# Four mod steps in the router of layer 0, f32r routing weights and tokens, and expert weights in 1 MB transfers of two rows per partition

## The chip, the cores and the metric

The kernel runs on one core of a Trainium2 chip. The time is the device time of one execution in microseconds, and what counts is the median of several runs: 1551.51 us over three runs (1550.75 to 1552.95) before the change.

## The reference, cut to what matters

A diffusion backbone of two layers over 256 latent tokens `x` and 256 context tokens `ctx`, with D = 1024. Layer 0 mixes tokens by windowed attention, layer 1 by differential attention, and behind each stands a hierarchical mixture of 32 experts (4 groups of 8, the best two in the best group). Layer 0 works on all 512 tokens, layer 1 needs the 256 latent ones alone. Shift, scale and gate of every sub-layer (`mod`) are products of `silu(c)` and `silu(c_ctx)` with `mod_w`.

```python
mod  = (silu(c)     @ mod_w[i] + mod_b[i]).reshape(B, 6, 1, D)     # modc from c_ctx
h = rmsnorm(x, norm_g[i, 1]) * (1 + mod[:, 4]) + mod[:, 3]
lg = t @ wg + bg                       # 4 groups
le = t @ we + be                       # 32 experts
top_p, top_i = top_k(softmax(le of the best group), 2)
wts = p_grp * top_p / sum(top_p)
u = xblk @ w_up[e]                     # w_up[e] is 1024 x 1024
y = (silu(u[:, :512]) * u[:, 512:]) @ w_down[e]      # w_down[e] is 512 x 1024
out[token] += wts * y
x = x + mod[:, 5] * out
```

All inputs are float32. The expert weights are 2 x 32 x 6.3 MB, all of which are read, whatever the routing is.

## The kernel before, in words

**Memory.** SBUF holds an arena of 43 slots of 128 x 1024 f32 (4 KB per partition each). `Slot` hands them out, the longest free first. `Stream.one` (L171 to 178) takes a slot and issues the next entry of `plan` as a DMA of 512 KB on SP's queue. SP runs ahead of the work: its next DMA waits until the slot's last reader is through, and until the DMA eight before it (they share eight semaphores in turn) has landed. So the order of `plan` is the order of the transfers, and how far they run ahead is the number of slots that the rest of the kernel leaves.

**The order of work.** TensorE's instructions stand in the order in which the code issues them (a manual schedule for that engine); the other engines get theirs from a scheduler at build time. What each engine does is then a fixed list, and it waits at the head of its list.

**Mod steps.** `mod_step` (L353 on, matmuls at L370) multiplies two k-tiles of one third of `mod_w` for `c` and `c_ctx`: four DMAs of 512 KB and 16 records of matmuls. Four steps make one third, then `mod_finish` copies the sums out of PSUM, transposes them and adds the bias. Layer 0's attention runs through 24 turns; every third of them carries a mod step (`MODS`), so eight steps lie there; the last four belong to the first third of layer 1 and stand in `plan` ahead of the attention's output weights `win_w_o`.

**The router.** `Post` normalises the tokens, transposes them to rows (`flip`, L917 and L925 to L929) and computes the logits (L950). `moe` (L982) then forms on VectorE, one short instruction behind the other (L990 to L1013), the 0/1 matrix `Mb` of token and expert. TensorE turns it into ranks (L1018) and counts (L1024); `key` (L1020) is the place of each token at its expert, 64 places (CAP) for each.

**A pair of experts.** 16 pairs per layer run through the same stages. `gather` (L1126): `P` (L1129) is the one-hot matrix of 128 places; two times `half` (L1152) multiplies `P` with the tokens, 512 features each; in layer 0 the tokens lie as two f32r parts (hi, lo), so that a half is 8 matmuls (4 tiles by 2 parts), in layer 1 as plain f32 (2 matmuls in two passes each, 4 records; `WHOLE`). L1168 transposes `P` for the way back. `gather_weights` (L1188) multiplies `P` in f32 with the routing weights `WR`, and VectorE copies the two or three columns out of PSUM (L1191, L1193). `spread_tokens` (L1198) transposes the gathered tokens, and L1200 adds the shift of `mod`. `up` (L1209) is 64 matmuls of 128 x 512 per pair, `gate` (L1216 to L1218) the SwiGLU, `turned` (L1240) its transpose, `down` (L1252) 32 matmuls, `weigh` (L1277, L1278) scales the output, and `combine` (L1291) with `gated_add` (L509) spreads the pair before back over the tokens while `up` runs. The last pair's `down_last` (L1264) is cut by columns, so that its output can be normalised and stored as it comes. At pair 5 a branch (L1085) asks whether an expert got more than 64 tokens; its other path does not run here.

In layer 0 the experts' stream has 31 slots, in layer 1 39. A pair's weights are 24 DMAs: 12.58 MB.

## Time and profile before

| | |
|---|---|
| median of 3 runs | 1551.51 us (1550.75 to 1552.95) |
| the profiled execution | 1550.44 us, of which its span 1548.8 us |
| TensorE busy | 1458.1 us (94%), granted clock 0.981 in the mean |
| VectorE, ScalarE, GpSimd busy | 42%, 25%, 12% |
| chain of work that ended last | TensorE above all; its costliest lines are L1209 and L1252 |
| bytes moved | 485.67 MB, mean 314 GB/s |
| layer 0, attention | to about 277 us |
| layer 0, router, then its 16 pairs | 282 to 300, then to about 815 us |
| layer 1, `up` of its first pair, of its last | from 1061.85 us, from 1507.87 us |

The span is that of the instructions; all times of rows count from its start. A row of the timeline gives the start, the length and the first and last words of a run of like instructions; "[8.10 <-DVE Mb L1013]" behind one is the idle time of its engine just ahead of it and what ended it. A length overlaps the next row's start where matmuls follow closely, so a stage is read from start to start.

### The profile page before, as it was taken

Reading aid. Unit: us, or ns where it says so; the run is one execution under the profiler, and the core shown is the slowest. Engines: PE = TensorE matmul, PEld = TensorE weight load, DVE = VectorE, ACT = ScalarE, POOL = GpSimd, SP = SyncE. Lnnn points to the kernel's source line nnn. Section 1 sums busy time; section 2 is a strip of 40 time slices with the busy share of each in tenths; the row PEclk is TensorE's granted clock in tenths of the full one; section 3 lists DMA queues with packets and bytes.
Section 4 is the critical chain, followed back from the end, with each engine's and each line's share of the span. In section 5 each row is a group of like instructions: output and inputs, shape, how many; then the busy total and the mean of one; then the engine's idle time right before and its main releaser. Section 6 shows DMA issues by size and latency. Waiting matters only on the chain. (4 is left out here: it accounts for less than half of the span.)

```text
span 1548.8 us, 20271 instructions
## 1 busy us (share of the span) xinstructions
PE 1458.1 (94%) x7463; PEld 800.3 (52%) x7463; DVE 655.5 (42%) x1585; ACT 384.6 (25%) x823; POOL 184.2 (12%) x147
## 2 busy tenths in 40 slices
PE   6998999799999999999999899798999899999997
PEld 4765567445444454444545678684434333433444
DVE  3338862424333443333448726863323222322323
ACT  4426653211010011101115235652101010110112
POOL 2314551000000000000006463100000000000000
PEclk9999999899999999999998999999999999999999
DMA  9767225799989999999996532488999999999991
GB/s 330 243 214 273 82 86 187 278 366 401 395 343 393 401 398 398 391 397 403 382 297 229 182 124 71 161 284 304 387 409 409 409 408 409 409 409 409 409 394 68
DMA packets 169695, 485.67 MB, mean 314 GB/s; under 512 B 20825, under 2 KB 41586, under 8 KB 169586
## 3 DMA queue, kind: packets, MB, share of 16 engines
q1 hardware_dynamic: 169088, 483.66, 82.2%
q8 instruction: 63, 1.03, 0.3%
q10 hardware_dynamic: 498, 0.60, 0.1%
q14 instruction: 46, 0.38, 0.1%
HBM read 483.16 MB, written 1.05 MB: 313 GB/s over the span
## 5 line engine op out<-in xcount | busy, mean ns | idle before, releaser
L1209 PE MATMUL ps<-slotf,row 128*64 128x512 f32 x2048 | 449.2, 593 | 2.1 <-DVE row L1200 2.1
L1209 PEld LDWEIGHTS ps<-slotf,row 128*64 128x64 f32 x2048 | 145.2, 137 | 289.7 <-issue 274.4
L1252 PE MATMUL ps<-slotf,row 128*64 128x512 f32 x960 | 212.6, 595 | 0.0
L546 PE MATMUL ps<-slotr,slotr 128*128 128x512 f32 x768 | 193.4, 405 | 13.4 <-DVE slotf L1414 6.7
L509 DVE SCALAR_TENSOR_TENSOR slotf<-ps,mod,slotf 128x256 f32<-128x256 f32 x408 | 167.3, 477 | 62.3 <-PE ps L1291 29.7
L546 PEld LDWEIGHTS ps<-slotr,slotr 128*128 128x128 f32 x768 | 145.1, 194 | 50.4 <-DVE slotf L1414 7.1
L1252 PEld LDWEIGHTS ps<-slotf,row 128*64 128x64 f32 x960 | 66.3, 137 | 124.9 <-issue 118.9
L1216 ACT ACTIVATE row<-ps 128x512 f32<-128x512 f32 x30 | 17.9, 597 | 425.9 <-PE ps L1209 386.6
L1217 DVE SCALAR_TENSOR_TENSOR row<-row,ps 128x512 f32<-128x512 f32 x30 | 20.6, 687 | 234.4 <-ACT row L1216 234.3
L1278 DVE SCALAR_TENSOR_TENSOR row<-ps,ty,row 128x512 fp32r<-128x512 f32 x60 | 45.0, 750 | 176.5 <-ACT row L1277 173.3
L1277 ACT ACTIVATE row<-ps,ty 128x512 fp32r<-128x512 f32 x60 | 41.3, 688 | 263.0 <-PE ps L1252 262.7
L1291 PE MATMUL ps<-row,row 128*128 128x512 f32 (+1 forms) x512 | 104.4, 348 | 1.1 <-DVE slotf L509 1.0
L1291 PEld LDWEIGHTS ps<-row,row 128*128 128x128 f32 x512 | 77.3, 189 | 36.5 <-ACT row L1216 21.1
L521 POOL TENSOR_TENSOR slotr<-slotf,slotr 128x1024 fp32r<-128x1024 f32 x32 | 78.9, 2479 | 86.9 <-ACT slotr L517 72.1
L1200 DVE TENSOR_TENSOR row<-ps,mod 128x512 f32<-128x512 f32 x64 | 42.7, 686 | 101.7 <-PE ps L1198 100.9
L481 POOL TENSOR_TENSOR row<-row,row 128x512 f32<-128x512 f32 (+1 forms) x13 | 15.0, 1156 | 575.6 <-PE ps L1291 519.4
L1152 PE MATMUL ps<-slotf,row 128*128 128x512 f32 x128 | 65.0, 632 | 7.0 <-PEq L1085 4.7
L1152 PE MATMUL ps<-slotr,row 128*128 128x512 f32 x256 | 70.4, 419 | 0.0
L517 ACT ACTIVATE slotr<-slotf 128x1024 fp32r<-128x1024 f32 x44 | 45.9, 1055 | 63.1 <-DMA slotf<-in_diff_w_qkv 38.0
L1152 PEld LDWEIGHTS ps<-slotr,row 128*128 128x128 f32 x256 | 47.9, 198 | 10.0 <-issue 0.8
L1377 PE MATMUL ps<-slotr,slotr 128*128 128x512 f32 x192 | 47.6, 399 | 0.0
L1198 PE MATMUL ps<-ident,row 128*128 128x128 f32 x256 | 37.8, 280 | 7.5 <-DVE row L1156 6.7
(314 smaller groups left out, 1526.8 us busy)
## 6 DMA issues: line engine op xcount, KB each, us to landing
slotf<-in_moe_w_up SPq DMA_DIRECT2D x512, 512.0 KB, 9.5
slotf<-in_moe_w_down SPq DMA_DIRECT2D x256, 512.0 KB, 10.2
slotf<-in_mod_w SPq DMA_DIRECT2D x96, 512.0 KB, 6.3
slotf<-in_diff_w_qkv SPq DMA_DIRECT2D x24, 512.0 KB, 3.9
slotf<-in_win_w_qkv SPq DMA_DIRECT2D x12, 512.0 KB, 5.2
slotf<-in_win_w_o SPq DMA_DIRECT2D x8, 512.0 KB, 4.0
slotf<-in_diff_w_o SPq DMA_DIRECT2D x8, 512.0 KB, 4.1
slotf<-in_x SPq DMA_DIRECT2D x2, 512.0 KB, 4.1
```

What stands on the lines that cost most here:

```text
L509: ve.scalar_tensor_tensor(xT[k][:, sl], ps[:, sl], g[:, k, r:r + 1], xT[k][:, sl], op0=OP.mult, op1=OP.add)
L517: se.activation(hv, v, AF.Copy)
L521: (eng or (ge if split_i[0] % 3 == 0 else ve)).tensor_tensor(lv, v, hv.bitcast(F32), op=OP.subtract)
L546: pe.matmul(ps[t], h[:, x, ts], w[y][:, kk, :], start=(k + kk == 0 and n == 0), stop=(k + kk == KT - 1 and n == 2))
L1152: pe.matmul(g, P[:, t, :] if len(tok[t]) > 1 else P[:, t, :].bitcast(F32), v[:, hs], start=(t == 0 and i == 0), stop=(t == nt - 1 and i == ...
L1200: ve.tensor_tensor(o.rearrange("p (k c) -> p k c", k=4), ps.rearrange("p (k c) -> p k c", k=4), mods[l][:, 3, 4 * h:4 * h + 4, 0:1].to_bro ...
L1209: pe.matmul(u[h][64 * s:64 * s + 64, :], st["xt"][k // 4][:, c0:c0 + 64], w[s][1][:, h * 512:(h + 1) * 512], start=(k == 0), stop=(k == KT ...
L1252: pe.matmul(y[h][64 * s:64 * s + 64, :], acT[:, c0:c0 + 64], w[s][1][:, h * 512:(h + 1) * 512], start=(k == 0), stop=(k == 3))
L1277: se.activation(yh, y[h], AF.Copy, scale=wsl)
L1278: ve.scalar_tensor_tensor(yl, y[h], wsl, yh.bitcast(F32), op0=OP.mult, op1=OP.subtract)
L1291: pe.matmul(out, part[:, c * 128:(c + 1) * 128], st["PT"][:, :T], start=(i == 0), stop=(i == 1))
L1377: pe.matmul(ps, w[x][:, k % 4, ms], oT0[k][1][:, y, :], start=(k == 0 and i == 0), stop=(k == KT - 1 and i == 2))
```

## The change

1. **Mod steps.** Four of the eight steps in layer 0's attention move into layer 0's router: three behind the logits and one around the counts (`mods_meanwhile`, `last_mods`), with the sums copied by ScalarE and turned after pair 0's gather. In `plan` the output weights now come ahead of these steps' 16 DMAs.
2. **Tokens in two parts.** Layer 1's tokens too are kept as two f32r parts, so a half of the gather is 4 f32r matmuls there. Its eviction needs a second part, on VectorE (L1009 of the new file), and two more slots.
3. **Routing weights in two parts.** `WR` and the token scale are kept as hi and lo in f32r; one pass of `P` gives both parts, and ScalarE adds them as it copies them out (`add_parts`).
4. **Expert weights.** One DMA brings 1 MB into two neighbouring slots: each partition gets 8 KB that lie in a row in HBM, the rows 8p + k (k = 2j, 2j + 1) of `w_up`, or 4p + k of `w_down`. The partitions' rows are 32 KB apart in `w_up` and 16 KB in `w_down`. (Before, each partition got one row of 4 KB, and 128 partitions read 512 KB in a row.) To match, the token's features are dealt to the k-tiles by 8 (`dealt`, `deal` in the evictions), `gate` writes its output with the columns dealt by 4, and the shift is turned by a transpose, a matmul and some short VectorE instructions per layer (`turned_shift`). `up` and `down` fetch for two k and free both slots after the second. The last pair's `w_down` stays in 512 KB DMAs by columns.
5. **Slots** are handed out so that neighbours stay together. The masks take one slot until the end of attention 0. The stream in layer 0 then has 15 pairs of slots, in layer 1 18.

```diff
-WHOLE = ((), (0, 1))
+WHOLE = ((), ())
...
-MODS = range(0, 24, 3)
+MODS = range(0, 24, 6)
...
     def plan_experts(l):
         for p in range(NE // 2):
-            for k in range(KT):
+            for j in range(KT // 2):
                 for s in range(2):
-                    plan.append((a["moe_w_up"][l, 2 * p + s, k * 128:(k + 1) * 128, :], (1024,)))
...
+                    w = a["moe_w_up"][l, 2 * p + s].rearrange("(p k) n -> p (k n)", k=KT)
+                    plan.append((w[:, j * 2048:(j + 1) * 2048], (2, 1024), True))
+            if p + 1 < NE // 2:
+                for j in range(2):
+                    for s in range(2):
+                        w = a["moe_w_down"][l, 2 * p + s].rearrange("(p k) n -> p (k n)", k=4)
+                        plan.append((w[:, j * 2048:(j + 1) * 2048], (2, 1024), True))
...
+    while len(todo) > KT // 2:
+        plan_mod(*todo.pop(0))
+    plan_out(a["win_w_o"][0])
     while todo:
         plan_mod(*todo.pop(0))
-    plan_out(a["win_w_o"][0])
     plan_experts(0)
...
-                cs = slice(ks[0] * 128, (ks[-1] + 1) * 128)
-                hs = slice(h * 512 + ks[0] * 128, h * 512 + (ks[-1] + 1) * 128)
+                src = deal(ps[:, ks[0] * 128:(ks[-1] + 1) * 128])
+                hs = 4 * h + ks[0], len(ks)
+                raw = dealt(self.slots[t][-1].f(), *hs)
                 if t < 2 and len(self.tok[t]) > 1:
...
+                    if self.nr == 1:
+                        ri = self.ri[:, t:t + 1]
+                        se.activation(hi, src, AF.Copy, scale=ri)
+                        ve.scalar_tensor_tensor(lo, src, ri, hi.bitcast(F32), op0=OP.mult, op1=OP.subtract)
...
+    def mods_meanwhile():
+        while len(mod_steps) > 1:
+            mod_step("A")
...
         with tc.manual_schedule(engines=PE):
             lg = post.logits()
+            mods_meanwhile()
...
+        moved = last_mods() if mod_steps else None
...
-                pe.matmul(wps[:, 0:1], P[:, t, :].bitcast(F32), ri[:, t:t + 1], start=(t == 0), stop=(t == nt - 1))
-                ve.tensor_copy(st["w"][:, 1:2], wps[:, 0:1])
+                    pe.matmul(wps[:, 0:2], P[:, t, :], ri[:, t, :], start=(t == 0), stop=(t == nt - 1))
+                add_parts(st["w"][:, 1:2], wps[:, 0:2])
...
+    def add_parts(dst, src):
+        n = src.shape[0]
+        se.activation(tiny("ap", [128, 2], bufs=2)[:n], src, AF.Copy, accum_out=dst)
+
     def gather_weights(P, WR, p, st, n):
...
-            pe.matmul(wps[:, 0:n], P[:, t, :].bitcast(F32), WR[:, t, p, 0:n], start=(t == 0), stop=(t == nt - 1))
+            pe.matmul(wps[:, 0:2 * c], P[:, t, :], WR[:, t, p], start=(t == 0), stop=(t == nt - 1))
...
-            ve.tensor_copy(st["w"][pb, 0:1], wps[pb, s:s + 1])
+            add_parts(st["w"][pb, 0:1], v[pb, s])
...
     def up(st, u, k):
-        w = [stream.next() for _ in range(2)]
+        if k % 2 == 0:
+            st["w_up"] = [stream.next() for _ in range(2)]
+        w = st["w_up"]
...
-        for s in range(2):
-            w[s][0].free()
+        if k % 2:
+            for s in range(2):
+                w[s][0].free()
```

The order of instructions is set at build time, so it can be read for both kernels. **TensorE in the router of layer 0.** The first list is the kernel before, from the last transpose of the tokens (`slotf` is a tile of them) over the logits to the ranks; `before_b` and `ones_b` are constants, `Mb` comes from VectorE.

```order
L917 MATMUL ps_2603<-ident,slotf_111 128x128
L950 MATMUL ps_2651<-ident,row_2633 128x36 x4
L1018 LDWEIGHTS before_b
L1018 MATMUL ps_2702<-Mb_2700,before_b 128x32
L1018 LDWEIGHTS ones_b
L1018 MATMUL ps_2702<-Mb_2700,ones_b 128x32
```

The next two are the changed kernel at the same place: its logits (L1037) with the first matmuls behind them, and the last ones ahead of the ranks (L1121). L419 is the matmul of a mod step, its first name the sums, its second a slot of `mod_w`.

```order
L1000 MATMUL ps_2613<-ident,slotf_65 128x128
L1037 MATMUL ps_2661<-ident,row_2643 128x36 x4
L419 MATMUL ps_2671<-slotf_91,slotf_69 32x512
L419 MATMUL ps_2671<-slotf_93,slotf_69 32x512
L419 MATMUL ps_2671<-slotf_111,slotf_69 32x512
```

```order
L419 MATMUL ps_2671<-slotf_59,slotf_69 32x512
L419 MATMUL ps_2671<-slotf_61,slotf_69 32x512
L419 MATMUL ps_2671<-slotf_95,slotf_69 32x512
L1121 LDWEIGHTS before_b
L1121 MATMUL ps_2749<-Mb_2747,before_b 128x32
```

Between the logits and the ranks there now stand 25 matmuls of mod steps, the last of which reads a fourth step's slot; seven more stand behind the counts.

**SP at the start of layer 0's experts.** Before, the transfers of the output weights and the first of the experts' (`in_moe_w_up`) alternate:

```order
L177 DMA slotf_81<-in_win_w_o 128x4x256
L177 DMA slotf_89<-in_moe_w_up 128x1024
L177 DMA slotf_81<-in_moe_w_up 128x1024
L177 DMA slotf_77<-in_moe_w_up 128x1024
L177 DMA slotf_83<-in_win_w_o 128x4x256
L177 DMA slotf_83<-in_moe_w_up 128x1024
```

and in the changed kernel the tail of the moved steps' weights (`in_mod_w`) stands around the first wide slot (`slotw`):

```order
L217 DMA slotf_89<-in_mod_w 128x2x512
L217 DMA slotf_73<-in_mod_w 128x2x512
L217 DMA slotw_197<-in_moe_w_up 128x2048
L217 DMA slotf_59<-in_mod_w 128x2x512
L217 DMA slotf_61<-in_mod_w 128x2x512
L217 DMA slotf_95<-in_mod_w 128x2x512
L217 DMA slotf_97<-in_mod_w 128x2x512
L217 DMA slotw_190<-in_moe_w_up 128x2048
```

The mod weights of the third step (`slotf_59`, `slotf_61`) and of the fourth (`slotf_95`, `slotf_97`) are issued behind that wide transfer, whose slots are free when attention 0's output product is done.

**VectorE in the router of layer 1.** Before, from the search for the best two to `Mb` and `key`:

```order
L1005 MAX_INDEX s_8330<-s_8329,row_8286 128x8 x2
L1006 TENSOR_SCALAR s_8331<-s_8330 128x16
L1010 TENSOR_TENSOR row_8286<-idx_211,s_8331 128x64
L1011 TENSOR_TENSOR row_8337<-idx_211,s_8331 128x64
L1013 TENSOR_TENSOR Mb_8340<-row_8286,row_8337 128x64
L1020 SCALAR_TENSOR_TENSOR key_8346<-ps_8342,Mb_8340 128x64
```

and changed:

```order
L1108 MAX_INDEX s_8282<-s_8281,row_8234 128x8 x2
L1109 TENSOR_SCALAR s_8283<-s_8282 128x16
L1009 SCALAR_TENSOR_TENSOR slotr_74<-ps_8239,ri_8210,slotr_72 128x8x64
L1009 SCALAR_TENSOR_TENSOR slotr_86<-ps_8246,ri_8210,slotr_84 128x8x64
L1009 SCALAR_TENSOR_TENSOR slotr_74<-ps_8253,ri_8210,slotr_72 128x8x64
L1009 SCALAR_TENSOR_TENSOR slotr_86<-ps_8260,ri_8210,slotr_84 128x8x64
L1113 TENSOR_TENSOR row_8234<-idx_271,s_8283 128x64
L1114 TENSOR_TENSOR row_8289<-idx_271,s_8283 128x64
L1116 TENSOR_TENSOR Mb_8292<-row_8234,row_8289 128x64
```

The four evictions of the tokens' second part stand ahead of the three instructions that end in `Mb`.

## Rows read from the trace of the kernel before

**Rows 1.** The page's line of TensorE: busy time, share of the span, instructions.

```profile
PE 1458.1 (94%) x7463; PEld 800.3 (52%) x7463; DVE 655.5 (42%) x1585; ACT 384.6 (25%) x823; POOL 184.2 (12%) x147
```

**Rows 2.** Busy time of each engine in four stretches: attention 0, the router of layer 0, pairs of layer 0, pairs of layer 1. Columns: the stretch and its length, then busy time and count of TensorE's matmuls, of its weight loads, of VectorE, ScalarE and GpSimd, the granted clock (1.00 is the higher of TensorE's two levels), and the DMA engines' busy share and rate in GB/s.

```profile
155.00:203.00 48.00, 48.00 (x342) 28.39 (x340) 39.36 (x110) 30.12 (x94) 25.82 (x24) 1.00 0.23 78
282.00:300.40 18.40, 8.06 (x48) 6.57 (x47) 14.62 (x60) 5.46 (x11) 2.52 (x2) 0.63 0.70 273
325.00:781.00 456.00, 449.39 (x2160) 215.67 (x2157) 170.81 (x379) 52.95 (x85) 0.00 (x0) 0.99 0.99 388
1100.00:1500.00 400.00, 387.77 (x1861) 166.54 (x1858) 117.72 (x247) 45.34 (x82) 0.00 (x0) 1.00 1.03 409
```

**Rows 3.** All matmuls of mod steps as one group (busy time, mean ns, idle time ahead), and TensorE's timeline in attention 0 at the start of two steps that follow each other (start, length, line, operands).

```profile
L370 PE MATMUL ps<-slotf,slotf 128*32 128x512 f32 x192 | 30.4, 599 | 0.0
```

```profile
179.96 1.04 PE L370 MATMUL ps<-slotf,slotf 128*32 128x512 f32 x2
...
191.89 1.05 PE L370 MATMUL ps<-slotf,slotf 128*32 128x512 f32 x2
```

**Rows 4.** TensorE's timeline from the ranks of layer 0 (the idle time ahead of them begins behind the logits) to the first `up`.

```profile
291.02 0.18 PE L1018 MATMUL ps<-Mb,before_b 128*128 128x32 bf16 x1 [8.10 <-DVE Mb L1013]
...
292.65 1.84 PE L1142 MATMUL ps<-ri,row 128*128 128x1 f32 x8 [1.09 <-DVE s L1031]
294.35 3.76 PE L1152 MATMUL ps<-slotr,row 128*128 128x512 f32 x8
...
300.38 1.94 PE L1209 MATMUL ps<-slotf,row 128*64 128x512 f32 x8 [0.78 <-DVE row L1200]
```

**Rows 5.** TensorE's timeline at the end of attention 0's output product, and SP's timeline of DMA issues around it (start, stretch over which they were issued, count).

```profile
275.21 2.32 PE L1377 MATMUL ps<-slotr,slotr 128*128 128x512 f32 x9
```

```profile
242.49 20.59 SPq L177 DMA_DIRECT2D slotf<-in_moe_w_up  x11
```

**Rows 6.** TensorE's timeline in one pair of layer 0, and the next pair's `down`.

```profile
615.70 7.09 PE L1252 MATMUL ps<-slotf,row 128*64 128x512 f32 x32
...
640.96 0.95 PE L1188 MATMUL ps<-WR,row 128*128 128x3 f32 x8
641.77 2.09 PE L1152 MATMUL ps<-slotr,row 128*128 128x512 f32 x8
644.16 0.63 PE L1168 MATMUL ps<-ident,row 128*128 128x128 f32 x4 [0.30 <-DVE ty L1193]
...
647.45 1.94 PE L1252 MATMUL ps<-slotf,row 128*64 128x512 f32 x8
```

**Rows 7.** VectorE's and ScalarE's timeline at the same place.

```profile
640.78 2.83 DVE L509 SCALAR_TENSOR_TENSOR slotf<-ps,mod,slotf 128x256 f32<-128x256 f32 x7
643.53 0.31 DVE L1191 COPY ty<-ps 64x1 f32<-64x1 f32 x2
643.86 0.16 DVE L1193 COPY ty<-ps 128x1 f32<-128x1 f32 x1
```

```profile
644.13 0.69 ACT L1162 ACTIVATE row<-ps,ty 128x512 f32<-128x512 f32 x1 [5.23 <-DVE ty L1193]
```

**Rows 8.** TensorE's timeline in one pair of layer 1, and the next pair's `up`.

```profile
1092.90 13.90 PE L1209 MATMUL ps<-slotf,row 128*64 128x512 f32 x64
...
1108.75 1.88 PE L1152 MATMUL ps<-slotf,row 128*128 128x512 f32 x4
...
1111.38 1.98 PE L1152 MATMUL ps<-slotf,row 128*128 128x512 f32 x4
...
1114.14 1.09 PE L1198 MATMUL ps<-ident,row 128*128 128x128 f32 x8 [0.44 <-DVE row L1156]
...
1122.09 2.31 PE L1209 MATMUL ps<-slotf,row 128*64 128x512 f32 x10
```

**Rows 9.** The router of layer 1: TensorE's timeline from the ranks to the first half of the gather, a short ScalarE instruction behind it; and from layer 0 a VectorE instruction of the form of the four new ones.

```profile
1055.04 0.18 PE L1018 MATMUL ps<-Mb,before_b 128*128 128x32 bf16 x1 [2.46 <-DVE Mb L1013]
...
1056.20 3.46 PE L1152 MATMUL ps<-slotf,row 128*128 128x512 f32 x4 [0.89 <-DVE s L1031]
```

```profile
1056.26 0.21 ACT L1036 ACTIVATE s<-s 128x8 f32<-128x8 f32 x1 [2.30 <-DVE s L1035]
```

```profile
295.33 0.75 DVE L974 SCALAR_TENSOR_TENSOR slotf<-slotf,s,slotf 128x512 f32<-128x512 f32 x1
```

**Rows 10.** DMA traffic of two stretches: 1100 to 1500 us (expert weights, rows of 4 KB) and 130 to 145 us (`mod_w`, rows of 2 KB). Packets and bytes, and by queue the time that its packets took as a share of 16 engines' time.

```profile
DMA packets 44886, 163.63 MB, mean 409 GB/s; under 512 B 4980, under 2 KB 5007, under 8 KB 44861
...
q1 hardware_dynamic: 44861, 163.29, 102.4%
```

```profile
DMA packets 2179, 4.23 MB, mean 282 GB/s; under 512 B 128, under 2 KB 128, under 8 KB 2176
...
q1 hardware_dynamic: 2176, 4.19, 77.6%
```

**Rows 11.** SP's issues of the last two pairs' `up` weights; the rate of all DMA from 1505 to 1525 us in 40 slices of half a us (the last weights land in the 23rd, at 1516.5); and TensorE's timeline at the last quarter of the last `down`.

```profile
1444.61 19.50 SPq L177 DMA_DIRECT2D slotf<-in_moe_w_up  x16
...
1475.30 20.67 SPq L177 DMA_DIRECT2D slotf<-in_moe_w_up  x16
```

```profile
GB/s 330 360 350 289 311 350 373 307 340 344 336 322 373 350 346 348 344 279 221 121 76 37 25 0 0 0 0 0 0 0 0 0 0 0 0 0 0 0 0 0
```

```profile
1533.60 1.95 PE L1264 MATMUL ps<-slotf,row 128*64 128x256 f32 x16
```

More of the change, by code (lines that the diff above doesn't have):

```diff
@@ L1090, in moe @@
                 if p == 0:
-                    st = gather(l, nt, 0, key, WR, tok, unit, weights, ri=post.ri)
+                    st = gather(l, nt, 0, key, WR, tok, unit, weights, ri=() if unit else rr)
+                    turn_mods()
+                    if moved:
+                        homes[l].slot.free()
                 if p != IF_AT:
@@ L1247, in down @@
         for k in range(4):
-            w = [stream.next() for _ in range(2)]
+            if k % 2 == 0:
+                w = [stream.next() for _ in range(2)]
             for h in range(2):
```

196 lines of the change are left out of this document (141 added, 55 removed).

## The prediction, made before the changed kernel ran

> **What bounds the kernel now.** I read the page's line of TensorE first: it is busy for 1458.1 of 1548.8 us [rows 1], so the path is TensorE's list nearly throughout, and an edit pays where it shortens that list or a wait in it. Then busy time by stretch [rows 2], because the 94% is a mean over stages with different limits. Attention 0 has TensorE busy for all of 48.00 us, with VectorE at 39.36, not far behind. The router of layer 0 is a hole: 8.06 busy of 18.40 us, and the granted clock falls to 0.63. The pairs of layer 0 run TensorE at 449.39 of 456 us while DMA moves 388 GB/s. The pairs of layer 1 have a second limit close by: 387.77 of 400 us for TensorE, and DMA engines that are never free (share 1.03) at 409 GB/s. A pair is 12.58 MB, 30.76 us at that rate; the issues of two pairs are 30.69 us apart [rows 11], while TensorE needs 1122.09 - 1092.90 = 29.19 [rows 8]. So DMA already loses 1.5 us per pair, and the kernel gets through because the stream starts layer 1 with 39 slots full. This decides the forecast: whatever TensorE gains in layer 1 counts only as far as DMA keeps up.
>
> **Attention 0.** The 12 mod steps are 192 records, 30.4 us [rows 3], so one is 2.53 and the four that leave are worth 10.1. Successive steps start 11.93 us apart [rows 3]; a period without a step is 9.40 on TensorE. VectorE works 39.36 of 48.00 us, 9.8 in such a period, which is longer, so a short period can be VectorE-bound by up to 0.4; but short and full periods alternate, and over two VectorE has 19.6 of TensorE's 21.3. I take **-8** (-10.1 to -5; the weak end is a VectorE that doesn't spread its work over two periods).
>
> **The hole in layer 0.** TensorE idles 8.10 us ahead of the ranks [rows 4]. Three steps are 7.6 and the fourth's first matmul about 0.3, so what is put there just fits. Their price is nothing as long as their weights are there. Those of steps 3 and 4 now stand on SP behind a 1 MB transfer that waits for the output product, which ends at 277.5 [rows 5]. That is 1.05 MB + 4 x 0.52 MB = 3.1 MB, 7.7 us at 409 GB/s, so the last is in at about 286 to 287; step 3 needs its part at 288.0 and step 4 at 290.5 (all less the shift of attention). Before, 11 expert transfers were out in that queue from 242.49 on [rows 5]; what follows these weights on SP, the other wide transfers, has until 300 for its first. Behind the counts stand 7/8 of a step, 2.2 us, in a gap of 1.09 [rows 4]: +1.1; the turn of the sums adds about 0.6. Against that, a TensorE that was busy should be granted more clock: the first half of the gather took 3.76 [rows 4] where the same 8 matmuls take 2.09 in a later pair [rows 6], -1.7, and L1142's eight records of 1.84 become four in one pass, at most 4 x 0.26 = 1.05 by that row, -0.8. The sum is -0.8; I take **0** (-2 to +2.5), since a late transfer or a full PSUM bank can only add.
>
> `turned_shift` adds per layer a transpose, a matmul and five VectorE instructions, about 1 us where nothing covers them (each 0.15 to 0.3 like L1191, [rows 7]). In layer 1 attention covers some: **+1** (0 to +2.5) for both. In the early stages the stream has a slot less, frees slots in twos, and starts layer 0 later: **+0.5** (-1.5 to +2.5).
>
> **Layer 0's pairs.** L1188 goes from 8 records in 0.81 us (640.96 to 641.77, [rows 6]) to 4; halves give -0.4, and 4 at 0.26, as for 512 columns, would give +0.2. Behind it the transposes of P wait 0.30 for L1193 [rows 6], because VectorE first finishes seven gated adds, 640.78 to 643.5, and then copies the weights out [rows 7]. ScalarE is idle there for 5.23 us [rows 7]; three adds at 0.21, the price of a short ScalarE instruction [rows 9], are through at 642.6, ahead of the first half's end at 643.86. So the wait goes. What is late next is the eviction of the tokens, which follows the half itself. That is 0.7 at best; I take 0.6 x 15 = **-9** (-10.5 to -5).
>
> **Layer 1's router.** The scheduler puts four evictions of the tokens' second part between the best-two search and `Mb`, for which TensorE already waits 2.46 [rows 9]. At 0.75 each, the same form in layer 0 [rows 9], that is +3.0, the whole of it on the path: behind them in VectorE's queue stand `Mb`, `key` and the one-hot, and TensorE has nothing else. In return the first half, 3.46 at the low clock [rows 9], halves nearly: -1.6. Together **+1.4** (0 to +3).
>
> **Layer 1's pairs.** A half is 1.88 and 1.98 us now [rows 8]; four f32r matmuls are half of the 2.09 of layer 0's eight [rows 6], 1.05. That is -1.76 per pair; I take 1.7. The shorter L1188 brings nothing: L1198 waits 0.44 for the eviction of the second half [rows 8] and would wait longer. The new `gate` has strided columns, and VectorE has time (117.72 of 400 us, [rows 2]). 15 x 1.7 + 0.9 for the first pair's second half: **-26.4**.
>
> **DMA.** Without it the first `up` of layer 1 comes at 1061.85 - 14.1 = 1047.8 (at 1061.85 before, table), and the end at 1508.3. What the transfers allow: 18 pairs of slots hold 1.5 pairs of experts, 14.5 remain, at x us each. Before, 1061.85 + 14.375 x 30.7 = 1503, and the last weights landed at 1516.5 [rows 11], so 13 us are lost at the start and with the small pieces of the end. The last quarter of `down` begins 15.2 before the end [rows 11]; with a wait for the landing I count 16. So the end is 1047.8 + 14.5x + 29. Now x. In 1100 to 1500 us 44861 - 4980 = 39881 rows of 4 KB took 102.4% of 16 x 400 us, 164.3 ns each; in 130 to 145 us 2176 - 128 = 2048 rows of 2 KB took 77.6% of 16 x 15 us, 90.9 ns each [rows 10]. So 2 KB more cost 73.4 ns, and a row of 8 KB 311 ns by estimate: 421 GB/s, or 431 if the 2.4% over full share overlap in the same way. No trace here has such rows at pitches of 16 and 32 KB; the lower end is 409, no gain from the length. I take 421, since it goes by counted time: x = 29.88, the end at 1510.1, just behind TensorE's 1508.3: **+2** (0 at 427 and over, where x is 29.5, and +14.5 at 409).
>
> The Trainium skill has a rule on this, "DMA: Bandwidth & Descriptors", Rules for kernel authors: transfers of 1 MiB and more for full bandwidth. Its table of measured bandwidth (section Bandwidth) gives 341 GB/s at 1 MB and 425 at 16 MB. The trace speaks against reading it by the size of one transfer: 512 KB ones in a row already move 409. By 425 GB/s x is 29.6, the last term +0.5 and the time 1511.5; by 341 x is 36.9, and the time by B's sum below about 1700; its chance is within B's.
>
> **Sum.** -8 + 0 + 1 + 0.5 - 9 + 1.4 - 26.4 + 2 = -38.5 on the span of 1548.8: 1510.3. The profiled execution is 1.6 longer than its span and the median of the runs 1.1 above that: **1513 us**.
>
> **Rivals.** *A: the length of rows brings nothing* (8 KB are fetched as two times 4 KB, or something behind the engines sets 409). Then x = 30.76 and the end is 1047.8 + 446 + 29 = 1522.8, time **1525.5**. For it: the same 409 in every part of that stretch; against it: the engines' own time is full, and it falls per byte from 2 KB to 4 KB rows. *B, slower than before: fetching at the wide pitch.* 128 partitions now read at addresses 32 KB apart instead of 512 KB in a row. If that lowers the rate, layer 1 follows x at once, and layer 0 from about 31.6 on (its TensorE period, 31.75 less 0.6, and what the lead covers), so the end is 571 + 30.5x. It is at 1548.8 for x = 32.1, 392 GB/s; at 375 GB/s (x = 33.5) it is 1593, time **1596**. Against it: `mod_w`, whose rows of 2 KB lie 24 KB apart, cost 90.9 ns each [rows 10], only 9 more than half a row of 4 KB in one piece. The Trainium skill's rule for it is in "DMA: Bandwidth & Descriptors", Latency and other measured facts: a row pitch at large powers of two falls from 214 to 207 GB/s at 512 KiB and 103 at 4 MiB. Its pitches are 16 times ours and more, and no row here shows one. *C: attention turns VectorE-bound and the moved weights come late*: -3 and +2.5 in place of -8 and 0, time **1520.5**. *D: the edit of the gather does not do what it says*: the f32r pair costs as much as the f32 passes, TensorE keeps 29.2 us; then 1513 - 2 + 26 = **1537**. Layer 0's rows of 2.09 for eight speak against it.
>
> **How the numbers follow.** Forecast 0.60, A 0.17, C 0.12, B 0.08, D 0.03. A measurement here tells 0.2%, 3 us, from no change. All but B are faster; a mild B is too or comes out even: faster 0.87, same 0.04, slower 0.09. Low end: attention -10.1, hole -2, pairs -10.5, early -1.5, DMA 0, 1508.3 - 8.1 + 2.7 = 1503, with 2 for what layer 1's wait may give: 1501. High end: A with C, 1533.
>
> **What would show it.** Right: layer-1 periods of about 27.5 at first and 29.9 where DMA sets them; 420 GB/s in 1060 to 1460; halves of 1.05; no idle ahead of the ranks in layer 0; an attention period pair of 21.3 to 22; 5 us of idle ahead of layer 1's ranks. Wrong: `up` waiting for slots by more than 5 us in all (A, B), below 392 GB/s (B), a wait of mod matmuls for DMA (C).

## The result and the profile after

The changed kernel takes **1528.59 us** (median of four runs) against 1551.76 us (four runs too): ratio 0.9847 [0.9827, 0.9866]. One of its four runs, 1686.91 us at a mean granted clock of 0.837, was slow; the ratio is that of the fast ones, 1526.76 to 1529.71. The forecast was 1513 in a range of 1501 to 1533: faster, and inside the range, but the gain on the span of the profiled executions is 20.8 us (1548.8 to 1528.0) where 38.5 were expected. So the question is which terms of the sum are missing 17.7 us.

I cut both spans at the same six places of TensorE's timeline: the end of attention 0's output product, the first `up` of layer 0, the first matmul of the norm behind layer 0's experts, the first matmul of the norm behind attention 1, the first `up` of layer 1, the end. The forecast by stage is put together from its terms; `turned_shift` (+1) is halved between the two attentions, the early stages' +0.5 stands in attention 1, and DMA's +2 in the last row. The last column is a second trace of the changed kernel, from run 9 below.

| stage | before | changed | difference | forecast | changed, run 9 |
|---|---|---|---|---|---|
| start to the end of attention 0 | 277.5 | 278.6 | +1.1 | -7.5 | 276.0 |
| router of layer 0 | 22.9 | 23.0 | +0.1 | 0 | 21.3 |
| pairs of layer 0 | 515.5 | 506.0 | -9.5 | -9 | 504.8 |
| attention 1 | 231.0 | 237.8 | +6.8 | +1 | 239.8 |
| router of layer 1 | 15.0 | 16.5 | +1.5 | +1.4 | 16.5 |
| pairs of layer 1, end | 487.0 | 466.1 | -20.9 | -24.4 | 467.2 |

The routers and layer 0's pairs came out to within half a us of the forecast. The loss is in the two attentions, 8.6 and 5.8 us, and 3.5 more in layer 1's pairs. Two traces of the same kernel differ by up to 2.6 us in a stage, so what is smaller than that isn't settled by one trace; the three losses stand in both.

**Attention 0.** Busy time of each engine in stretches of the changed kernel, against [rows 2] with the same columns: attention 0, the router and the pairs of layer 0, the pairs of layer 1.

```profile
155.00:203.00 48.00, 46.42 (x315) 28.00 (x313) 39.20 (x111) 31.06 (x98) 24.49 (x24) 1.00 0.03 12
282.00:300.40 18.40, 16.85 (x111) 7.44 (x108) 14.16 (x63) 7.01 (x18) 2.55 (x2) 0.81 1.02 420
325.00:770.00 445.00, 442.14 (x2095) 210.49 (x2095) 170.76 (x338) 65.17 (x168) 0.00 (x0) 0.99 1.00 408
1100.00:1470.00 370.00, 353.81 (x1780) 158.64 (x1778) 112.47 (x208) 51.62 (x130) 0.00 (x0) 0.99 1.01 421
```

What TensorE waits for from 155 to 222 us (us in all, times, longest):

```profile
PE ps L844 <- POOL slotf L841: 2.9, 6, 0.9
PE ps L837 <- DVE ty L819: 1.1, 1, 1.1
PE ps L837 <- ACT slotf L848: 0.8, 1, 0.8
```

And busy time in the last turns alone:

```profile
203.00:221.00 18.00, 14.08 (x99) 8.92 (x99) 13.59 (x36) 10.61 (x32) 8.28 (x8) 1.00 0.32 103
```

Before, TensorE had no idle time in 155 to 203 us [rows 2]; now it has 1.58, and 3.92 of 18 in the last turns. No engine is full there (VectorE 39.20 of 48 us, GpSimd 24.49). The waits are short ones, between steps of a turn that hand on to each other: TensorE's transposes wait for GpSimd's L841, VectorE's L819, ScalarE's L848. Before, all of TensorE's waits from 155 to 222 us came to 0.6 us. Where a mod step stood between such steps before, nothing does now.

**The router of layer 0** is filled as planned: the hole of 8.10 us [rows 4] holds the fifty matmuls, and in this trace the ranks wait for nothing.

```profile
284.56 8.76 PE L419 MATMUL ps<-slotf,slotf 128*32 128x512 f32 x50
293.24 0.19 PE L1121 MATMUL ps<-Mb,before_b 128*128 128x32 bf16 x1
...
293.69 1.92 PE L419 MATMUL ps<-slotf,slotf 128*32 128x512 f32 x14
...
301.61 3.65 PE L1334 MATMUL ps<-slotw,row 128*64 128x512 f32 x16 [0.60 <-DVE row L1323]
```

The fifty took 8.76 us here, at a granted clock of 0.70 (284.6 to 293.2 us). In run 9 the clock of the whole router is 1.00, they take 6.20, and 1.50 us of the hole are left:

```profile
281.34 6.20 PE L419 MATMUL ps<-slotf,slotf 128*32 128x512 f32 x50
289.03 0.18 PE L1121 MATMUL ps<-Mb,before_b 128*128 128x32 bf16 x1 [1.50 <-DVE Mb L1116]
```

**A pair of layer 0**, against [rows 6]: the routing weights' matmuls stand 0.36 us ahead of the half instead of 0.81, and the wait of 0.30 behind the half is gone.

```profile
636.15 0.51 PE L1310 MATMUL ps<-WR,row 128*128 128x6 f32 x4
636.51 2.09 PE L1269 MATMUL ps<-slotr,row 128*128 128x512 f32 x8
638.44 0.60 PE L1285 MATMUL ps<-ident,row 128*128 128x128 f32 x4
```

**A pair of layer 1**, TensorE's timeline, against [rows 8]: the halves (L1269) are half as long, the wait ahead of the token transposes is longer (0.81 against 0.44), and it ends at ScalarE's L1303, an add of the routing weights (`add_parts`), not at the eviction as before.

```profile
1107.01 1.09 PE L1269 MATMUL ps<-slotr,row 128*128 128x512 f32 x4
1107.94 0.38 PE L1285 MATMUL ps<-ident,row 128*128 128x128 f32 x2
...
1108.85 1.20 PE L1269 MATMUL ps<-slotr,row 128*128 128x512 f32 x4
1109.88 0.28 PE L1310 MATMUL ps<-WR,row 128*128 128x4 f32 x2
1110.97 1.09 PE L1321 MATMUL ps<-ident,row 128*128 128x128 f32 x8 [0.81 <-ACT ty L1303]
```

The eviction of the second half (VectorE) and the last add (ScalarE) in the same pair, and the eviction before the change:

```profile
1110.08 0.69 DVE L1273 COPY row<-ps 128x512 f32<-128x512 f32 x1 [0.27 <-PE ps L1269]
1110.72 0.20 ACT L1303 ACTIVATION_READ_ACCUMULATOR ty<-ps 64x1 f32 x1
```

```profile
1113.40 0.69 DVE L1156 COPY row<-ps 128x512 f32<-128x512 f32 x1 [2.12 <-PE ps L1152]
```

**Attention 1.** SP's issues, VectorE and TensorE near 880 us: the last three of the 32 `mod_w` transfers are issued at 873.04 and from 881.43 on; before, the last seven were out by 870.1. VectorE waits 10.30 us for the first of the three, and 3.24 for the others; before, it waited for none. The copy L1544 out of PSUM, which stands behind the first on VectorE, holds up TensorE.

```profile
873.04 0.42 SPq L217 DMA_DIRECT2D slotf<-in_mod_w  x1
...
881.43 0.93 SPq L217 DMA_DIRECT2D slotf<-in_mod_w  x2
```

```profile
859.48 10.61 SPq L177 DMA_DIRECT2D slotf<-in_mod_w  x7
```

```profile
878.78 3.50 DVE L1659 SCALAR_TENSOR_TENSOR slotf<-slotf,keep,slotf 128x512 f32<-128x512 f32 x2 [10.30 <-DMA slotf<-in_mod_w]
882.19 1.28 DVE L1544 COPY slotf<-ps 128x512 f32<-128x512 f32 x2
```

```profile
882.93 29.42 PE L598 MATMUL ps<-slotr,slotr 128*128 128x512 f32 x120 [6.11 <-DVE slotf L1544]
...
997.60 0.48 PE L905 MATMUL ps<-row 8*128 8x128 f32 x2 [1.50 <-DVE row L901]
```

TensorE waited for that copy before the change too. The whole of it from 800 to 1050 us, before (L1414) and changed (L1544), is 4.1 us more:

```profile
PE ps L546 <- DVE slotf L1414: 6.7, 1, 6.7
```

```profile
PE ps L598 <- DVE slotf L1544: 10.8, 2, 6.1
```

**DMA** from 1100 to 1470 us, against [rows 10]:

```profile
DMA packets 21356, 155.70 MB, mean 421 GB/s; under 512 B 2367, under 2 KB 2367, under 8 KB 2367
...
q1 hardware_dynamic: 21333, 155.38, 101.0%
```

### The profile page after: what moved, and what is told of

It reads as the page before. It is cut to its first block, busy times and chain, and to the rows that moved or that the text cites. A ratio compares the mean times of both kernels' runs of the same rounds, so it can differ in the third digit from the quotient of the medians.

```text
span 1528.0 us, 19467 instructions
## 1 busy us (share of the span) xinstructions
PE 1431.6 (94%) x7369; PEld 795.0 (52%) x7369; DVE 663.9 (43%) x1522; ACT 410.8 (27%) x986; POOL 184.7 (12%) x147
## 5 line engine op out<-in xcount | busy, mean ns | idle before, releaser
L1334 PE MATMUL ps<-slotw,row 128*64 128x512 f32 x2048 | 449.6, 593 | 2.6 <-DVE row L1323 2.6
L1334 PEld LDWEIGHTS ps<-slotw,row 128*64 128x64 f32 x2048 | 145.3, 137 | 290.3 <-issue 279.8
L1380 PE MATMUL ps<-slotw,row 128*64 128x512 f32 x960 | 212.6, 595 | 0.0
L598 PE MATMUL ps<-slotr,slotr 128*128 128x512 f32 x768 | 193.3, 405 | 17.4 <-DVE slotf L1544 10.8
L598 PEld LDWEIGHTS ps<-slotr,slotr 128*128 128x128 f32 x768 | 145.1, 194 | 54.9 <-DVE slotf L1544 11.6
L1380 PEld LDWEIGHTS ps<-slotw,row 128*64 128x64 f32 x960 | 66.3, 137 | 124.9 <-issue 124.1
L1343 DVE SCALAR_TENSOR_TENSOR row<-row,ps 128x512 f32<-128x512 f32 x30 | 20.6, 688 | 233.7 <-ACT row L1342 233.6
L1269 PE MATMUL ps<-slotr,row 128*128 128x512 f32 x384 | 108.8, 420 | 7.5 <-PEq L1199 4.5
L1323 DVE TENSOR_TENSOR row<-ps,shift 128x512 f32<-128x512 f32 x64 | 42.7, 686 | 105.9 <-PE ps L1321 105.9
L1269 PEld LDWEIGHTS ps<-slotr,row 128*128 128x128 f32 x384 | 70.2, 196 | 28.2 <-PEq L1199 4.7
L569 ACT ACTIVATE slotr<-slotf 128x1024 fp32r<-128x1024 f32 x44 | 45.8, 1055 | 70.9 <-DMA slotf<-in_diff_w_qkv 16.5
L1321 PE MATMUL ps<-ident,row 128*128 128x128 f32 x256 | 38.3, 282 | 13.0 <-ACT ty L1303 12.3
L1321 PEld LDWEIGHTS ps<-ident,row 128*128 128x128 f32 x256 | 28.6, 142 | 30.7 <-issue 13.8
## 6 DMA issues: line engine op xcount, KB each, us to landing
slotf<-in_moe_w_down SPq DMA_DIRECT2D x16, 512.0 KB, 10.1
```

The lines of the kernel that those rows point to most:

```text
L569: se.activation(hv, v, AF.Copy)
L598: pe.matmul(ps[t], h[:, x, ts], w[y][:, kk, :], start=(k + kk == 0 and n == 0), stop=(k + kk == KT - 1 and n == 2))
L1269: pe.matmul(g, P[:, t, :] if len(tok[t]) > 1 else P[:, t, :].bitcast(F32), v[:, hs], start=(t == 0 and i == 0), stop=(t == nt - 1 and i == ...
L1321: pe.transpose(ps[:, k * 128:(k + 1) * 128], st["x"][h][:, k * 128:(k + 1) * 128], ident)
L1323: ve.tensor_tensor(o.rearrange("p (k c) -> p k c", k=4), ps.rearrange("p (k c) -> p k c", k=4), moe_shift[l][:, 4 * h:4 * h + 4].unsqueeze ...
L1334: pe.matmul(u[h][64 * s:64 * s + 64, :], st["xt"][k // 4][:, c0:c0 + 64], w[s][1][:, k % 2, h * 512:(h + 1) * 512], start=(k == 0), stop=( ...
```

## The experiments

Ratios are against runs of the kernel before on the same chip; runs 1 to 4, 5 to 8 and 9 to 10 share a chip.

**1. Rows of 4 KB in transfers of 1 MB.** The neighbouring rows are given up, the size of a transfer stays.

```diff
-                    w = a["moe_w_up"][l, 2 * p + s].rearrange("(p k) n -> p (k n)", k=KT)
-                    plan.append((w[:, j * 2048:(j + 1) * 2048], (2, 1024), True))
+                    w = a["moe_w_up"][l, 2 * p + s, j * 256:(j + 1) * 256]
+                    plan.append((w.rearrange("(q p) n -> p q n", p=128), (2, 1024), True))
...
```

The same is done for `w_down`, the features and `gate`'s columns are no longer dealt, and the plain shift overwrites the turned one (one short copy more per layer).

> The changed kernel with the row order of the weights undone: still 1 MB per transfer into two neighbouring slots, but each partition gets two rows of 4 KB that lie 512 KB apart, the features are not dealt, and the turned shift is formed and then overwritten by the plain one (one short copy per layer more). If the length of rows makes the rate (my theory), layer 1 falls back from 421 to about 409 GB/s; the last weights land at first up + 14.5 x 30.76 + 13 = about 1521 in place of 1508, behind the point at which the last quarter of down could start (1512.8), and the time is 8 to 10 us above the changed kernel's 1526.8 to 1529.7. If the size of a transfer makes it, the rate stays at 421 and the time equal within 2 us. If the dealt evictions or the dealt gate cost time, the pairs' periods (31.08 and 27.75 us) become shorter; I expect them equal within 0.05.

1535.88 us, 0.9923 [0.99, 0.9946]: 7.3 above the changed kernel by the medians; in the trace the pairs of layer 1 take 477.6 us against 466.1. The periods of pairs that don't wait for weights are 31.08 and 27.75 us as in the changed kernel, so dealing the features costs them nothing. DMA from 1100 to 1470 us, and what TensorE and its weight loads wait for from 1055 us on:

```profile
DMA packets 39188, 151.29 MB, mean 409 GB/s; under 512 B 2308, under 2 KB 2308, under 8 KB 39165
```

```profile
PE ps L1335 <- DMA slotw<-in_moe_w_up: 6.6, 6, 1.5
PEld ps L1335 <- DMA slotw<-in_moe_w_up: 13.8, 13, 2.4
```

The rate is that of the 512 KB transfers before, 409, and waits for weights appear. So the layout of the rows makes the rate, not the size of the transfer; the length of the rows and the distance between them changed together.

**2. The mod steps back.** All else as in the changed kernel.

```diff
-MODS = range(0, 24, 6)
+MODS = range(0, 24, 3)
...
-    while len(todo) > KT // 2:
+    while todo:
         plan_mod(*todo.pop(0))
     plan_out(a["win_w_o"][0])
-    while todo:
-        plan_mod(*todo.pop(0))
     plan_experts(0)
```

> The changed kernel with all eight mod steps in attention 0 again and their weights ahead of the output weights, all else kept. My theory now: a step split in pieces between other work costs nearly as much as before for every piece (a first piece alone takes 1 us whatever it holds), so the move saved little in attention and the mods fill an idle hole that then costs the same: attention from its first to its last matmul stays within 2 us, the router gets its idle 8 us and its slow gather back at equal length, and the time stays within 3 us of the changed kernel's. The rival, by which attention did gain and something else took it (the order of slots, the output weights): this run is 4 to 8 us slower.

1539.14 us, 0.9936 [0.992, 0.9953]: 10.5 slower than the changed kernel by the medians, as if the four steps had been worth their whole 10.1 us. But the stages don't put it on the steps. The 24 turns of attention, from the first matmul of a turn (118.64) to the last (220.99), take 102.4 us with eight steps; before 102.1 (121.53 to 223.67), in the changed kernel 99.1 (122.06 to 221.14). So four steps are worth 3.1 to 3.3 us there. (The turns begin 3.4 us earlier here than in the changed kernel's trace, but 0.6 earlier than in run 9's, at 119.22: their start varies.) 5.2 us come behind the turns, where VectorE's L947 ran long once (4.94 us for three), TensorE waited, and the granted clock was 0.79 from 226 to 242 us (1.00 in the changed kernel):

```profile
229.69 2.04 PE L950 MATMUL ps<-row,ones 128*128 128x512 f32 x2 [2.74 <-DVE row L947]
230.74 11.23 PE L1505 MATMUL ps<-slotr,slotr 128*128 128x512 f32 x37
```

The same 37 matmuls take 8.98 in the changed kernel. Another 4.7 us lie in the period of layer 1 with the branch at pair 5 (39.4 against 34.7 us; 34.4 to 38.3 in the other runs of the changed kernel and its variants). Why either place ran longer here is open. The hole of layer 0, empty again (7.60 us ahead of the ranks), costs 21.5 us with its router, and 21.3 to 21.7 in the other runs where it is filled: filling it is free.

**3. The stream's slots, attention 1 only.** The changed kernel hands out whole pairs of slots first, to the stream too; here, from attention 1 on, a single slot is the longest free, as before (`oldest` is filled in `start1`, where attention 1 begins).

```diff
+    oldest = []
...
-                    pairs = whole_pairs()
+                    pairs = [] if oldest else whole_pairs()
...
     def start1():
+        oldest.append(1)
```

> The changed kernel with one thing taken back in attention 1: a slot for the stream is the one that has been free longest, as in the kernel before, and not the first of the pair that has been free longest. If the new order of slots holds up the late mod weights (theory: SP waits for a reader that ends late, VectorE then waits 10.3 us for that transfer, and the copies that free TensorE's banks stand behind it), that wait and TensorE's 6.1 us go, and the time falls by 5 to 7 us, to about 1522. If the stage simply has fewer slots, or the transfers come late for another reason, the wait stays and the time is equal within 2 us.

1528.79 us, 0.9865 [0.984, 0.9889]: no change. VectorE's wait for the late `mod_w` falls from 13.5 to 4.6 us, but TensorE still waits 8.5 for the copy L1544 (L1545 here), in one wait instead of 10.8 in two. Alone the rule for single slots makes no difference that can be measured.

**4. Layer 1's tokens in f32.** This run leaves out the tokens' scale in layer 1.

```diff
-WHOLE = ((), ())
+WHOLE = ((), (0, 1))
```

> The changed kernel with layer 1's tokens in plain f32 again, two matmuls in two passes per half, without the second evictions in the router. Theory: the two halves cost 0.79 us each more, so the pairs go from 27.75 to about 29.3; the router of layer 1 is 2 to 3 us shorter up to Mb and loses 1 to 1.6 in its first half. Together 15 x 1.5 + 0.8 - 1.5 = +22, time about 1550. Rival: the wait for ScalarE's copy of the routing weights (0.8 us per pair) would have been there anyway and the gain in the halves is smaller: +15 or less.

1552.91 us, 1.0019 [1.0009, 1.0028]. From the first `up` of layer 1 to the end 489.9 us against 466.1: 23.8 us, all of it in the periods (29.33 against 27.75 us, 15 times 1.58). The f32r halves are the whole gain of layer 1; without them the other parts of the change together are 0.2% slower than the kernel before. The period is 0.15 longer than the 29.18 before the change, though the halves are the same: the transposes wait 0.81 for ScalarE's L1303 here too. The router gets no shorter (17.4 us), since its first half runs at the low clock again, 3.75 us.

**5. Oldest slots for all, the weights' splits too.** `split` asks for two neighbouring slots in the changed kernel; here both it and the stream take the longest free.

```diff
-                    pairs = whole_pairs()
+                    pairs = []
...
-        hi, lo = buddies()
+        hi, lo = Slot(at=free[0]), Slot(at=free[0])
```

> The changed kernel with the slots handed out as before wherever a single one is asked for and for the split weights: the one that has been free longest (the wide transfers still take whole pairs). Theory: in both attentions the pairing rule gives the split weights and the stream slots whose last reader ends late. In attention 0 the output weights are split only after the last head's values (219.9 us), so the output product can no longer fill the gaps of the last heads; with the oldest slots it starts at 214 to 216 in place of 221.5 and ends 3 to 5 us earlier. In attention 1 the late mod weights come in time and the stage takes 231 to 234 in place of 237.9. Time 1518 to 1522. Rival: the slot that the masks take and the turned shift are what delays both stages; then the time stays within 2 us of 1528.6.

1521.8 us, 0.9819 [0.9803, 0.9835]: below the interval of run 9, the changed kernel again (0.985 to 0.988), and touching that of its first runs (0.9827 to 0.9866). The output product starts earlier, and in attention 1 VectorE no longer waits for DMA. SP's issues there, and TensorE at the product L598:

```profile
849.48 9.08 SPq L217 DMA_DIRECT2D slotf<-in_mod_w  x5
```

```profile
852.20 51.68 PE L598 MATMUL ps<-slotr,slotr 128*128 128x512 f32 x216 [8.27 <-DVE slotf L1544]
```

Attention 1 is 233.6 us instead of 237.8 and 239.8 in the two traces of the changed kernel; every other stage is within 0.5 us of run 9's. So the pairing of slots made the mod weights late.

**6. Oldest slots for the splits only** (the second half of 5's edit).

> The changed kernel with the oldest free slots for the two parts of split weights alone (the stream and the rest keep the pairing rule). Theory: part of the gain of the run before, in attention 0 above all: the output product starts 2 to 4 us earlier; the late mod weights of attention 1 stay late, since the stream's slots follow the pairs. Time 1523 to 1527. Rival as there: within 2 us of 1528.6.

1554.36 us, 1.004 [1.0024, 1.0057]: missed by 30 us, all up to the end of attention 0, at 308.8: 10.2 us ahead of the turns, 5.0 in them and 15.0 behind. What TensorE waits for at its output product, the issue of the last of its eight weight transfers, and that of the last three in the changed kernel:

```profile
PE ps L1507 <- ACT slotr L569: 11.9, 2, 6.1
```

```profile
284.53 0.37 SPq L217 DMA_DIRECT2D slotf<-in_win_w_o  x1
```

```profile
218.90 7.93 SPq L217 DMA_DIRECT2D slotf<-in_win_w_o  x3
```

My reading is that the splits now break up the whole pairs that the stream insists on, so that its transfers wait for slots. By the three runs the two rules belong together: both old or both new.

**7. As 5, with the tokens' second parts of layer 1 taken behind `Mb`, `key` and the one-hot** (four evictions that stand ahead of `Mb` on VectorE).

```diff
-                        ve.scalar_tensor_tensor(lo, src, ri, hi.bitcast(F32), op0=OP.mult, op1=OP.subtract)
+                        self.late.append(partial(ve.scalar_tensor_tensor, lo, src, ri, hi.bitcast(F32), op0=OP.mult,
+                                                 op1=OP.subtract))
...
         def weights():
+            for f in post.late:
+                f()
```

> The oldest slots everywhere as in the first run, and in layer 1's router the four evictions of the tokens' second part behind Mb, key and the one-hot in VectorE's list. Theory: Mb comes 3.0 us earlier; the first half of the gather then waits for two of these evictions, 1.5, so the first up comes about 1.5 us earlier than in the first run, and since the pairs of layer 1 are TensorE's, so does the end: 1.5 below the first run (0 to 2.5). Rival: the transfers are level with TensorE in layer 1, so nothing of it arrives at the end.

1523.91 us, 0.9825 [0.9808, 0.9841]: the router is 15.4 us instead of 16.5, but the pairs behind it take 469.2 instead of 467.1, and the time can't be told from 5's.

**8. As 1, without the turned shift.** Since 4 KB rows need no reordered features, the shift can be read as it lies.

```diff
     def logit_bias(l, nr):
-        turned_shift(l)
+        moe_shift[l] = mods[l][:, 3, :, 0]
```

> Weights in 1 MB transfers of two 4 KB rows as in the run of that kind before, and the turned shift not formed at all (with rows in their plain order it isn't needed). What it tells is the price of the turned shift. Theory: 2 to 3 us in attention 1, where TensorE waits 1.5 for its VectorE copy and the work behind it bunches, and 0 to 1 in attention 0; the time is 2 to 4 us below that run's 1535.9. Rival: other work covers it, and the time is equal within 1.5.

1533.55 us, 0.9897 [0.988, 0.9913], 2.3 below run 1 by the medians (on different chips; the ratios overlap). In the traces, from the last matmul of the turns to the end of the output product 55.7 us (217.86 to 273.6) against 57.6 (219.17 to 276.8), and attention 1 234.5 against 236.3: 1.9 and 1.8 us. The first of the two is 57.5 to 57.6 in run 1, run 3 and both traces of the changed kernel; attention 1 varies by 2 us between those two, so its 1.8 is less sure.

**9. The changed kernel again.**

> The changed kernel itself once more, with more rounds, beside the next one. 1526.8 to 1529.7 before; expected the same, with the same waits: VectorE for late mod weights in attention 1, 10 us, and the output product of attention 0 not before 219 us.

1528.71 us, 0.9865 [0.985, 0.988]. The turns take 99.4 us, from there to the product's end 57.5, VectorE waits 13.4 for `mod_w`, and attention 1 is 239.8: the two losses are there again.

**10. As 5, with the turned shift earlier**: layer 0's behind turn 8 of attention, layer 1's where the third of `mod` that it needs is finished.

```diff
     for i, _ in enumerate(run):
         mod_run(i in MODS)
+        if i == 8:
+            turned_shift(0)
...
     def logit_bias(l, nr):
-        turned_shift(l)
...
+        if done[0][0] == 3:
+            turned_shift(1)
```

> The oldest slots everywhere (as in the run of that name, 1521.8), and the turned shift formed as soon as its mods are there: in attention 0 after the ninth turn, in attention 1 with the first late mods, not with the bias of the logits. Theory: the shift was paid where TensorE had nothing to put beside it, 3.2 us at the end of attention 0 and 1.9 in attention 1 by the run without it; formed early it lies beside other work, and the time is 2 to 5 us below that run, 1517 to 1520. Rival: its short VectorE instructions delay the heads wherever they stand, or the transfers of layer 1, level with TensorE, take the gain: within 1.5 of 1521.8.

Median 1518.7 us over five runs (1515.33 to 1525.78), 0.9819 [0.98, 0.9839]. It beats the kernel before and the changed one (run 9, same chip, by 10 us), but its ratio can't be told from run 5's. In the trace attention 1 takes 230.3 us, as before the change (231.0). TensorE's product there waits 1.56 instead of 8.27; the shift's own two TensorE steps (L891, L896), now ahead of it, wait 1.4 and 2.5 us, where L905 waited 1.5:

```profile
850.26 49.28 PE L598 MATMUL ps<-slotr,slotr 128*128 128x512 f32 x216 [1.56 <-DVE slotf L1545]
```

## Why the prediction was right or wrong

The forecast of a gain holds, and the time is inside the range, but it is there in part by luck: 1528.6 lies nearer to rivals A (1525.5) and C (1520.5) than to 1513, and the range reached that far because its high end was A with C. Of neither did the cause occur. What is missing was lost in the two attentions above all; C had priced the first, by another cause, and no rival the second.

**Attention 0, -8: wrong, the step that the weak end leaned on.** I priced the four steps at their matmuls, 10.1 us, and let VectorE's *share* of time limit the gain. The turns gained 3.1 (3.3 by run 2). The rest turned into waits: in 130 to 225 us the mod matmuls fell from 20.7 to 12.6 us and TensorE's idle time rose from 1.8 to 7.1 (busy time by stretch, 23.85 + 24.00 + 24.00 + 21.38 of 95 us before, 23.48 + 23.54 + 22.88 + 17.98 now). 8.1 less work and 5.3 more idle leave 2.8. Rival C had the size (-3) but not the cause: the releasers are GpSimd's L841 most often, then VectorE and ScalarE, all far from full. So what limits seems to be the time from step to step within a turn, not the load of an engine; that is read from the waits and not shown by a run, as more turns in flight (`LAG0`) were not tried. Two periods with one step take 22.74 us (155.75 to 178.49), not the 21.3 to 22 that I named as the sign. The weights were not late, as C had them.

Behind the turns 3.6 us are lost (57.5 from their end to the product's, against 53.9). 1.9 is the turned shift (run 8). The other 1.7 would fit the product's start. Before, its first eight matmuls stood in the gaps of the last turns (TensorE's timeline of the kernel before):

```profile
214.79 1.17 PE L1377 MATMUL ps<-slotr,slotr 128*128 128x512 f32 x4
215.89 0.63 PE L785 MATMUL ps<-ident,row 128*128 128x128 f32 x4
216.27 0.71 PE L1377 MATMUL ps<-slotr,slotr 128*128 128x512 f32 x2
216.83 0.63 PE L785 MATMUL ps<-ident,row 128*128 128x128 f32 x4
217.22 0.70 PE L1377 MATMUL ps<-slotr,slotr 128*128 128x512 f32 x2
```

Now it begins at 221.47, because ScalarE splits its weights from 219.94 on. But run 5 starts it at 209.97 and ends it at 276.4, no earlier than run 9 (276.0): an earlier start alone gave nothing there, and the cause of the 1.7 stays open.

**The turned shift, +1: too small.** 1.9 and 1.8 by the traces of runs 1 and 8, 3.7 in all, above the upper end of 2.5. I counted seven short instructions by their durations; what counts is that they form a chain across TensorE and VectorE, at a place where nothing else is to be done (L905 waits 1.50 for VectorE). I had left layer 1's to be covered by attention; it isn't, until it is issued earlier (run 10).

**Early stages and slots, +0.5: wrong by its largest amount, in attention 1.** I thought of a slot less and a later start of layer 0. What happened is that the rule of whole pairs, for the single slots and for the splits together, delays `mod_w` for layer 1 (issued at 873.04 and later), and VectorE, waiting for it, holds up the copies that TensorE needs: 10.8 us of waits where there were 6.7. Run 5 undoes both rules: DMA's wait is gone, attention 1 is 4.2 and 6.2 us shorter than in the two traces of the changed kernel, and the time falls by 0.46% against run 9 by the ratios. Run 3 (the single slots alone) does nothing, run 6 (the splits alone) makes it worse. What is left after run 5, L598's wait of 8.27, is 1.6 more than before the change; it went with the earlier shift in run 10. That the shift is its cause was not tried apart, and the medians don't tell the two runs apart.

**The hole, 0: right.** The granted clock was 0.81 in that stretch instead of 0.63, as hoped, with 0.1 us more for the stage; the weights came in time. In run 9, at a clock of 1.00, the stage is 1.5 us shorter than before, and in run 2, with the hole empty, 1.4: what it gains doesn't come from the filling.

**Pairs of layer 0, -9: right.** A period went from 31.75 to 31.08, 0.67 where 0.6 was taken: 0.45 ahead of the half and 0.46 behind it, 0.30 of which was the wait, less some 0.2 that come back at the second half.

**Router of layer 1, +1.4: right, part by part.** The ranks wait 4.97 instead of 2.46, the first half takes 2.05 instead of 3.46 (TensorE's timeline; the four f32r matmuls still start at the low clock, 0.57 granted from 1056.1 to 1062 us):

```profile
1056.10 0.19 PE L1121 MATMUL ps<-Mb,before_b 128*128 128x32 bf16 x1 [4.97 <-DVE Mb L1116]
...
1057.21 2.05 PE L1269 MATMUL ps<-slotr,row 128*128 128x512 f32 x4 [0.81 <-DVE s L1141]
```

**Pairs of layer 1, -26.4: the mechanism right, the size off.** A period went from 29.18 to 27.75, 1.43 instead of 1.7. I took a half by the length of its group, 1.88 and 1.98; the group's end is modelled and runs into the next one. From start to start a half was 1.72 and 1.82 before (1108.75 to 1110.47, 1111.38 to 1113.20) and is 0.93 and 1.03 now (1107.01 to 1107.94, 1108.85 to 1109.88): 1.58 for both. 0.15 of it go to the place behind, from the start of the weights' matmuls to that of the token transposes, 1.09 against 0.94. The eviction of the second half doesn't make the difference: it ends 0.89 us behind the start of the weights' matmuls in both kernels (1110.77 and 1114.09, from the rows above), and before, the transposes began 0.05 later. Now they begin 0.05 behind the last of ScalarE's adds, which ends at 1110.92. So the routing weights' new way out, which gains 0.67 per pair in layer 0, costs 0.15 per pair in layer 1, 2.3 us over 15; run 4, with the old halves, shows the same 0.15. I had written that the shorter L1188 brings nothing here and set no price on the adds behind it.

**DMA, +2: the rate right, the bound not reached.** 421 GB/s was the forecast and the measurement; by the same count (101.0% of 16 x 370 us over 21356 - 2367 = 18989 rows of 8 KB) a row took 315 ns, where 311 was worked out. With the first `up` at 1061.9 instead of 1047.8, the transfers allow an end at 1061.9 + 14.5 x 29.88 + 29 = 1524.2 by the same formula, and TensorE ends at 1528.0, with a period of 27.75 to the last pair: DMA never set it, and the term is 0. Two slips in the prediction's working change nothing here: by its formula the bound falls below TensorE's 1508.3 from 423 GB/s on, not 427, and the terms of its low end add up to 7.6, not 8.1. Run 1 shows how close rival A was: at 409 the last periods are 28.14, 30.69 and 31.09 and 7 us are lost by the medians. The Trainium skill's rule for full bandwidth ("DMA: Bandwidth & Descriptors", Rules for kernel authors: 128 partitions and at least 1 MiB per DMA) is met by run 1 and by the changed kernel alike, 409 and 421 GB/s; so by these runs it isn't what tells them apart. B did not occur: no rate fell at pitches of 16 and 32 KB. D neither: run 4 is where it would have ended, at 1552.91.

## What to carry to other kernels

Work that is taken out of a full engine's list need not come back as time: 10.1 us of matmuls gave 3.1 to 3.3 here, with no other engine full. Look at the chain of steps within one turn, not only at the busy share of the other engines, before you price it. A step that moves to an idle engine can become the one that ends last, as ScalarE's adds did in layer 1. A rule on which memory a stream takes next is a rule on when each transfer starts, so follow the last transfer of each small, urgent tensor through it. Price a group of pipelined matmuls from its start to the next one's start, and a short chain of setup work by where it stands, not by its instructions.

## What the runs showed of the hardware

Rows of 8 KB, 16 and 32 KB apart, move at 421 GB/s, rows of 4 KB side by side at 409, both with transfers of 1 MB and DMA engines that are never free; the 12 GB/s decided 7 us of 1529 by the medians.

A wait of TensorE costs more than its own length when the granted clock falls behind it. In run 2 the 37 matmuls behind a wait of 2.74 us took 11.23 instead of 8.98 us: the wait cost nearly as much again. In the changed kernel the same stands behind L598's wait of 6.11 us in attention 1, where ten matmuls ran in the first 4 us and 19 in the next 4 (the clock is the third number from the end):

```profile
883.00:887.00 4.00, 4.00 (x10) 3.13 (x11) 0.76 (x2) 0.00 (x0) 2.37 (x1) 0.50 0.99 354
887.00:891.00 4.00, 4.00 (x19) 3.33 (x18) 2.73 (x4) 1.32 (x2) 0.51 (x1) 0.99 1.03 390
```
